# Two neighbouring rows per partition in the experts' weight tiles, and attention scores of two heads by turns

## The chip, the cores and the metric

The kernel runs on one core of a Trainium2 chip. The metric is the device time of one execution in microseconds (us). Engines are named as in the profile: PE is the matrix engine and PEld its weight loads (LDWEIGHTS), DVE the vector engine, ACT the scalar engine, POOL the GpSimd, SP the engine that issues most DMAs. A core has 16 DMA engines.

## The reference

All data is float32, batch 1, 256 tokens of 1024 channels beside a context of 256 tokens. A first block (Fourier mixer and state-space mixer) is followed by a second block of two layers, and it is the second block that the change touches:

```
for l in range(2):                      # layer 0 also updates the context stream, layer 1 does not
    sh1, sc1, g1, sh2, sc2, g2 = split(silu(c) @ ada_w[l] + ada_b[l], 6)   # the same for the context
    h  = rms_norm(x, norm_mix[l]) * (1 + sc1) + sh1
    x  = x + g1 * (even_layer if l == 0 else odd_layer)(h, hc)
    h2 = rms_norm(x, norm_ffn[l]) * (1 + sc2) + sh2
    x  = x + g2 * expert_choice_ffn(h2, router[l], w1[l], w3[l], w2[l])
...
even_layer:  4 differential heads (two softmaxes each, over 64 channels) and 8 neighbourhood heads of 64
             channels with an added bias; queries of x see keys of x and of the context, those of the context its own
odd_layer:   8 latent-attention heads, and 4 retention heads of 64 key and 128 value channels
expert_choice_ffn:   16 experts, each takes its 32 best tokens of a stream
    hid = silu(xe @ w1[e]) * (xe @ w3[e]);   ye = (hid @ w2[e]) * gate      # w1, w3, w2 are 1024 x 1024
```

Three matrices of 4 MiB for each of 16 experts in two layers make 384 MiB of weights, each read once: that is 403 MB of the 557 MB that the kernel moves.

## The kernel before

The program is one long list of Python generators that are woven into each other (`weave`), after which a scheduler orders each engine's instructions. SP issues the weight loads in program order; a load waits until the buffer that it fills has been read.

**Experts** (`moe`, from L1144). For each expert, `ffn` (L1256) multiplies the 32 chosen tokens by a 1024 x 1024 matrix. `load_m` (L1242) brings the matrix as four tiles of 1 MiB, `w` [128 partitions, 2, 1024], where partition p of tile `kk` holds rows 128·2kk + p and 128·(2kk+1) + p of the matrix: two runs of 4 KiB that lie 512 KiB apart in memory. PE keeps the tokens (`lhs`, columns of `xe`, `xf` or `hidT`) and streams the weights. In layer 0 the 64 columns of two streams are kept (x and context) and the array's columns serve two halves of the output, in layer 1 it is 32 columns and four quarters. Buffers for these tiles come from every pool that is free at the time (`slots`), about 20 of them.

The tokens that an expert reads, with their channels on partitions, are gathered by matmuls (`gather`, L1187): 128 channels of x, scaled, are the kept operand, and a 0/1 matrix is streamed. Channel block k is columns 128k to 128k + 127. Each block is then scaled and shifted by columns that `ada` (L359) computed. After w1 and w3, `hid` is transposed on PE in blocks of 128 columns (L1309) to be the kept operand for w2. `route` (L1081) transposes x in the same blocks for the router's logits.

**Even layer** (`even_attend`, L1370). It runs first for the context (`Qc`), woven with the projections of x, then for x (`Qx`), woven with the context's output projection. `scores` (L1375) multiplies the queries of one head, 64 partitions, by the keys: head 2ch + half lies on partitions 64·half to 64·half + 63, so that its matmul uses one half of the array's rows. For x there are two matmuls per head (own keys, context keys), and for a neighbourhood head a third, over all 128 rows, that adds the bias between the two. Then come the row maximum on DVE, the exponential on ACT, PE transposes and the matmul with the values.

**Ada** (`ada`): in the second block 12 calls per layer, each with two weight tiles [128, 4, 512] (runs of 2 KiB) and 32 matmuls on quarters of the array's columns.

**Prologue** (`late_rows`, L324): ten small DMAs issued by POOL and three PE transposes turn gain and bias vectors into columns (`VC`, `CV`; `BC` holds the ada biases).

Of the kernel before, what the change touches and what calls it, by code (L numbers as in the profile page):

```python
# [113 lines left out]
def kernel(ctx, tc, A, out, dbg=None):  # L114
# [25 lines left out]
    def psa():  # L140
        return ps_("a")
# [6 lines left out]
    def mm(o, l, r, start=True, stop=True, **kw):  # L148
        PE.matmul(o, l, r, start=start, stop=stop, **kw)  # L149
# [132 lines left out]
    v2 = pp.tile([128, 2, 128], F32, name="v2")  # L282
    v4 = pp.tile([128, 128], F32, name="v4")

    def rows_in(t, r0, ap, eng=G):
# [38 lines left out]
    def late_rows():  # L324
# [14 lines left out]
        V.tensor_copy(CV, p[:, 0:200])  # L339

    def vcol(name, i):
        c = VCI[name] + i
        return VC[:, c:c + 1]
# [5 lines left out]
    def ada_early(l, s, slots):  # L349
# [3 lines left out]
        for b in range(2):  # L353
# [3 lines left out]
            early[l, s].append(w)  # L357

    def ada(src, s, pair, cols, bias, between=None, bank=None, ws=None):  # L359

        p = (bank or psa)()
        for b in range(2):
            w = ws[b] if ws else load_w(src, [(s * 512, 512)], k0=4 * b, k=4)
            if between and b == 0:
                between()
            for k in range(4):
                for j in range(4):
                    mm(p[32 * j:32 * j + 32, 0:128], SC[:, 4 * b + k, pair, :], w[:, k, 128 * j:128 * j + 128],
                       start=b == 0 and k == 0, stop=b == 1 and k == 3)
# [142 lines left out]
    with tc.issue_after(after):  # L512
        late_rows()
    now(c2)
    pro.close()
# [541 lines left out]
    def router_rows(l):  # L1057
        nc.sync.dma_start(RW[l], A["moe_router_2"][l].rearrange("(k p) n -> p k n", p=128))

# [21 lines left out]
    def route(l, s, src, at="a", tag="b", jt="b"):  # L1081
# [5 lines left out]
        for kk in range(4):  # L1087
            xT = rowp.tile([128, 512], F32, name="xT", tag="r")
            p = ps_(TB[s])
            for j in range(2):  # L1090
                for t in range(2):
                    tr(p[:, 256 * j + 128 * t:256 * j + 128 * t + 128],
                       src[:, t, (2 * kk + j) * 128:(2 * kk + j + 1) * 128])
            if kk in (2,):
# [49 lines left out]
    def moe(l, streams, stk):  # L1144
# [42 lines left out]
        def gather(s, part, k, n=1):  # L1187
# [3 lines left out]
            if k % n == 0:  # L1191
                c = slice(128 * k, 128 * k + 128 * n)
                if n == 1:
# [48 lines left out]
        def load_m(src, k0, apart=False):  # L1242

            if not slots["first"]:
                slots["first"] += slots["all"]
            pool, tag = slots["first"].pop(0)
            w = pool.tile([128, 2048], F32, name="wm", tag=tag).rearrange("p (k n) -> p k n", k=2)
            sv = src.rearrange("(k p) n -> p k n", p=128)
            if apart:
                for k in range(2):  # L1250
                    nc.sync.dma_start(w[:, k], sv[:, k0 + k])
            else:
                nc.sync.dma_start(w, sv[:, k0:k0 + 2])
            return w
# [13 lines left out]
        def run():  # L1268
# [27 lines left out]
            for e in range(16):  # L1296
# [73 lines left out]
    def even_attend(st, Q, Y, nb_t=None):  # L1370
# [18 lines left out]
        for t in range(2):  # L1389
# [3 lines left out]
            for h in range(4):  # L1393
                pr = []
                for c in range(2):
                    ps = psa()
                    scores(ps, 0, h, c, qs)
                    pr.append(softmax_p(l2, ps, n, 1.0, "pr"))

# [17 lines left out]
            su8 = sm.tile([128, 8], F32, name="su8")  # L1417
            for h in range(8):
                ps = psa()
# [262 lines left out]
    def retention():  # L1682
# [11 lines left out]
        ps = psa()  # L1694
        for h in range(4):
            o = 64 * (h % 2)
            for d in range(2):
                c = 128 * (2 * d + h // 2)
                for t in range(2):
                    mm(ps[o:o + 64, c:c + 128], kw[:, t, d, 64 * h:64 * h + 64], rv[:, 2 + t, 128 * h:128 * h + 128],  # L1700
                       start=t == 0, stop=t == 1)
# [3 lines left out]
        for h in range(4):  # L1705
            o, a_ = slice(64 * (h % 2), 64 * (h % 2) + 64), h // 2
            ps = psa()
            for j in range(2):
                mm(ps[:, 256 * j:256 * j + 256], rkT[o, a_, 128 * j:128 * j + 128], rqT[o, a_, :])
            V.tensor_tensor(D[:, h], ps, D[:, h], op=OP.mult)  # L1710
            yield
        for t in range(2):
            qs = slice(128 * t, 128 * t + 128)
            cr = rs_.tile([128, 2, 2, 2, 128], F32, name="cr")
            for par in range(2):
                o = slice(64 * par, 64 * par + 64)
                ps = psa()
                for a_ in range(2):
                    for d in range(2):
                        c = 128 * (2 * d + a_)  # L1720
                        mm(ps[:, c:c + 128], rqT[o, a_, qs], sst[o, d, a_, :])
# [110 lines left out]
```

## Time and profile before

| | us |
|---|---|
| median of 3 executions | 1906.96 (1906.41 to 1912.91) |
| the profiled execution's own time | 1906.99 |
| its span, first to last instruction | 1905.1 |
| PE busy / DVE busy / ACT busy / POOL busy | 1652.3 / 794.4 / 519.3 / 335.1 |

The page of the profile lists 382 loads of 1024 KB for the experts' tiles and 4 of 512 KB, 18.4 us each (median) from issue to landing. The span falls into these stretches, by the tiles in use: first block to about 460 us, context attention to 600, x's attention to 740, experts of layer 0 from 760 to 1230, odd layer to 1430, experts of layer 1 from 1440 to 1892.

How to read it: a matmul of float32 operands stands in the trace as two records. A record's duration covers the array's depth too, so records overlap, and it is the distance between their starts that counts. "idle before" names what an engine waited for. The granted clock of PE is 1.00 for 2.4 GHz and 0.50 for 1.2 GHz, a mean over the stretch.

### The profile page before, as it was taken

Reading aid. Unit: us, or ns where it says so; the run is one execution under the profiler, and the core shown is the slowest. Engines: PE = TensorE matmul, PEld = TensorE weight load, DVE = VectorE, ACT = ScalarE, POOL = GpSimd, SP = SyncE. Lnnn points to the kernel's source line nnn. Section 1 sums busy time; section 2 is a strip of 40 time slices with the busy share of each in tenths; the row PEclk is TensorE's granted clock in tenths of the full one; section 3 lists DMA queues with packets and bytes.
Section 4 is the critical chain, followed back from the end, with each engine's and each line's share of the span. In section 5 each row is a group of like instructions: output and inputs, shape, how many; then the busy total and the mean of one; then the engine's idle time right before and its main releaser. Section 6 shows DMA issues by size and latency. Waiting matters only on the chain.

```text
span 1905.1 us, 29062 instructions
## 1 busy us (share of the span) xinstructions
PE 1652.3 (87%) x12036; PEld 1026.2 (54%) x12036; DVE 794.4 (42%) x1563; ACT 519.3 (27%) x1042; POOL 335.1 (18%) x288
## 2 busy tenths in 40 slices
PE   5999999899999998999989997789998966666665
PEld 4877777799887676433323322278784522222221
DVE  4538798947546655322323121164743300000002
ACT  4335555636443442211200000062532200000001
POOL 3114553633413310000000000041300000000001
PEclk8999999999999999999999999999997976776767
DMA  9576544555576539899989999951397999999996
GB/s 343 198 233 219 173 148 141 170 190 190 186 235 168 187 139 382 300 373 409 409 338 409 409 409 409 402 163 71 126 352 273 408 408 409 409 409 409 409 409 274
DMA packets 223016, 557.11 MB, mean 292 GB/s; under 512 B 23531, under 2 KB 80199, under 8 KB 222884
## 3 DMA queue, kind: packets, MB, share of 16 engines
q1 hardware_dynamic: 216608, 547.92, 76.9%
q10 hardware_dynamic: 5732, 6.26, 1.0%
q8 instruction: 95, 1.56, 0.3%
q0 software_dynamic: 544, 1.06, 0.1%
q14 instruction: 37, 0.30, 0.0%
HBM read 554.16 MB, written 1.05 MB: 291 GB/s over the span
## 4 chain that ended last, share of the span: by engine, by line
PE 60%; DMA 26%; DVE 8%; ACT 3%; issue 2%; POOL 1%; SPq 0%; DVEq 0%; POOLq 0%; ACTq 0%
PE ps_a L149 48%; DMA wm<-in_moe_w_dram 22%; PE ps_b L149 7%; PE ps_b L256 3%; DMA w<-in_w_in_dram 2%; DVE w L800 1%; PE ps_g L149 1%; DMA w<-in_w_ada_dram 1%; DVE wh L205 1%; ACT wh L203 1%; DMA w<-in_w_out_dram 1%; DVE ye L1323 1%; DVE pr L1404 1%; DVE hid L1305 1%; DVE acc L614 1%
## 5 line engine op out<-in xcount | busy, mean ns | idle before, releaser
L149 PE MATMUL ps_a<-wm,xf 128*32 128x256 f32 (+1 forms) x1792 | 280.0, 558 | 73.6 <-DMA wm<-in_moe_w_dram 71.8
L149 PE MATMUL ps_a<-wm,hidT 128*32 128x256 f32 (+1 forms) x1536 | 211.8, 529 | 47.4 <-DMA wm<-in_moe_w_dram 31.7
L149 PEld LDWEIGHTS ps_a<-wm,xf 128*32 128x32 f32 (+1 forms) x1792 | 90.4, 138 | 255.9 <-issue 133.3
L203 ACT ACTIVATE wh<-w 128x1024 fp32r<-128x1024 f32 (+3 forms) x152 | 151.7, 1007 | 164.6 <-PE ps_a L149 99.9
L1305 DVE TENSOR_TENSOR hid<-hid,ps_a 128x512 f32<-128x512 f32 (+1 forms) x32 | 17.7, 555 | 375.2 <-PE ps_a L149 375.2
L205 POOL TENSOR_TENSOR wh<-w,wh 128x1024 fp32r<-128x1024 f32 (+3 forms) x50 | 116.0, 2321 | 304.4 <-ACT wh L203 278.5
L205 DVE TENSOR_TENSOR wh<-w,wh 128x1024 fp32r<-128x1024 f32 (+3 forms) x102 | 135.2, 1329 | 71.9 <-ACT wh L203 71.4
L149 PEld LDWEIGHTS ps_a<-wm,hidT 128*32 128x32 f32 (+1 forms) x1536 | 70.4, 133 | 158.6 <-issue 74.8
L1323 DVE TENSOR_TENSOR ye<-ps_a,SC 32x512 f32<-32x512 f32 (+1 forms) x128 | 70.8, 553 | 193.9 <-PE ps_a L149 192.3
L1303 ACT ACTIVATE hid<-ps_a 128x512 f32<-128x512 f32 (+1 forms) x32 | 15.7, 490 | 480.9 <-PE ps_a L149 458.8
L149 PE MATMUL ps_a<-hT,wh 128*128 128x512 f32 (+1 forms) x672 | 136.3, 359 | 6.6 <-ACT hT L496 5.0
L1222 POOL TENSOR_TENSOR Pg<-Pg,CV 128x128 f32<-128x128 f32 x24 | 9.5, 421 | 748.7 <-DVE Pg L1220 748.7
L149 PEld LDWEIGHTS ps_a<-hT,wh 128*128 128x128 f32 x672 | 110.9, 197 | 25.9 <-ACT hT L496 5.4
L149 PE MATMUL ps_a<-E,wh 128*128 128x256 f32 x768 | 102.3, 288 | 6.1 <-DVE wh L205 2.5
L149 PE MATMUL ps_a<-wm,xe 128*32 128x256 f32 (+1 forms) x768 | 104.3, 481 | 0.7 <-ACT hid L1303 0.5
L149 PEld LDWEIGHTS ps_a<-E,wh 128*128 128x128 f32 x768 | 95.1, 192 | 12.6 <-issue 3.2
L149 PE MATMUL ps_a<-wh,E 128*128 128x256 f32 (+1 forms) x576 | 100.9, 326 | 0.1
L149 PEld LDWEIGHTS ps_a<-wh,E 128*128 128x128 f32 x576 | 81.5, 188 | 12.6 <-issue 5.0
L149 PE MATMUL ps_a<-wm,ye 128*32 128x256 f32 x512 | 51.6, 543 | 25.5 <-DMA wm<-in_moe_w_dram 25.5
L614 DVE SCALAR_TENSOR_TENSOR acc<-ps_a,CV,acc 128x189 f32<-128x189 f32 (+2 forms) x160 | 66.7, 427 | 8.2 <-ACT acc L603 5.7
L1023 ACT ACTIVATE pr<-ps_a,nb 128x512 f32<-128x512 f32 (+1 forms) x80 | 48.0, 601 | 76.0 <-DVE nb L1020 63.8
L149 PE MATMUL ps_a<-w,SC 128*32 128x128 f32 x1728 | 64.4, 281 | 2.7 <-DMA w<-in_w_ada_dram 2.1
(525 smaller groups left out, 2416.4 us busy)
## 6 DMA issues: line engine op xcount, KB each, us to landing
wm<-in_moe_w_dram SPq DMA_DIRECT2D x382, 1024.0 KB, 18.4
w<-in_ada_w_dram SPq DMA_DIRECT2D x46, 1024.0 KB, 5.8
w<-in_even_w_in_dram SPq DMA_DIRECT2D x24, 1024.0 KB, 6.4
w<-in_w_ada_dram SPq DMA_DIRECT2D x12, 1024.0 KB, 8.9
w<-in_w_in_dram SPq DMA_DIRECT2D x8, 1024.0 KB, 7.4
w<-in_even_w_out_dram SPq DMA_DIRECT2D x8, 1024.0 KB, 6.8
w<-in_w_in_dram SPq DMA_DIRECT2D x12, 512.0 KB, 7.3
w<-in_w_in_dram SPq DMA_DIRECT2D x8, 768.0 KB, 4.4
```

Source lines behind the costliest of these rows:

```text
L149: PE.matmul(o, l, r, start=start, stop=stop, **kw)
L203: S.activation(hv, wv, AF.Copy)
L205: (G if flip_lo[0] == 0 else V).tensor_tensor(lo, wv, hv, op=OP.subtract)
L256: PE.transpose(o, i, ident[:n, :n])
L614: V.scalar_tensor_tensor(o, xi[:, r0 + dr:r1 + dr, c0 + dc:c1 + dc], tap(i, j), o, op0=OP.mult, op1=OP.add)
L800: V.scalar_tensor_tensor(w[:, r], cb[:, c, 1], dt[:, c, 24 + h:25 + h], w[:, r], op0=OP.mult, op1=OP.add)
L1023: S.activation(pr[:, :n], ps[:, :n], AF.Exp, bias=nb, scale=scale, accum_out=su)
L1222: G.tensor_tensor(g_, g_, bcast(AFF[s][:, t, e4, None], [128, 4, 32]), op=OP.mult)
L1303: S.activation(hid, p1[:, :N], AF.Silu)
L1305: V.tensor_tensor(hid, hid, p3[:, :N], op=OP.mult)
L1323: V.tensor_tensor(ye[o:o + 32, s, N * j:N * j + N], py[i:i + 32, :N], G2[i:i + 32, :], op=OP.mult)
L1404: V.scalar_tensor_tensor(pr[0][0][:, :n], pr[1][0][:, :n], rc, pr[0][0][:, :n], op0=OP.mult, op1=OP.add)
```

## The change

The rows of the experts' matrices are dealt out in another way: partition p of a tile holds rows 256m + 2p and 256m + 2p + 1, which is one run of 8 KiB. The channels that meet them must then be taken two apart, which `in_pairs` does in the gather, the hidden transposes and the router's transposes; the shift and scale columns are made in that order by `ada` for four of the twelve calls per layer, and their biases, the gain and the router's rows by new small loads (`pair_rows`, `router_rows`). In the even layer and in retention the matmuls of two heads are issued by turns, one on each half of the array's rows.

```
+    def pair_rows():                       # called behind late_rows(), in the prologue
+        ab = A["ada_b_2"]
+        for l in range(2):
+            rows_in(v5, 8 * l, ab[l:l + 1, 3072:5120].rearrange("o (m c) -> (o m) c", c=256))
+        rows_in(v5, 16, A["norm_ffn_2"].rearrange("l (m c) -> (l m) c", c=256))
+        p = psb()
+        for i in range(2):
+            tr(p[:, 24 * i:24 * i + 24], v5[:, i::2])
+        pv = p[:, 0:48].rearrange("p (i r) -> p i r", i=2)
+        for l in range(2):
+            V.tensor_copy(BC[:, 48 + 48 * l:64 + 48 * l].rearrange("p (m i) -> p i m", i=2), pv[:, :, 8 * l:8 * l + 8])
+        V.tensor_copy(VC[:, o:o + 16].rearrange("p (m i) -> p i m", i=2), pv[:, :, 16:24])
+    def in_pairs(j, n=128):
+        c = 256 * (j // 2) + j % 2
+        return slice(c, c + 2 * n - 1, 2)
...
     def ada(src, s, pair, cols, bias, between=None, bank=None, ws=None):
+        paired = pair == 1 and 6 <= s < 10
-                    mm(p[32 * j:32 * j + 32, 0:128], SC[:, 4 * b + k, pair, :], w[:, k, 128 * j:128 * j + 128],
+                    mm(p[32 * j:32 * j + 32, 0:128], SC[:, 4 * b + k, pair, :],
+                       w[:, k, in_pairs(j) if paired else slice(128 * j, 128 * j + 128)],
...
     def router_rows(l):
-        nc.sync.dma_start(RW[l], A["moe_router_2"][l].rearrange("(k p) n -> p k n", p=128))
+        nc.sync.dma_start(RW[l].rearrange("p (m i) n -> p m (i n)", i=2), A["moe_router_2"][l].rearrange("(m p i) n -> p m (i n)", p=128, i=2))
...
     def route(...):
-                    tr(p[:, 256 * j + 128 * t:256 * j + 128 * t + 128],
-                       src[:, t, (2 * kk + j) * 128:(2 * kk + j + 1) * 128])
+                    tr(p[:, 256 * j + 128 * t:256 * j + 128 * t + 128], src[:, t, in_pairs(2 * kk + j)])
...
         def gather(s, part, k, n=1):
-                c = slice(128 * k, 128 * k + 128 * n)
+                c = in_pairs(k) if n == 1 else slice(128 * k, 128 * k + 128 * n)
...
-                    c = 128 * (k % n)
-                    mm(ps, pair[s][i][:, t, c:c + 128], Ps[s][:, t], start=t == 0 and i == 0, stop=t == 1 and i == 1)
+                    c = slice(0, 128) if n == 1 else in_pairs(k % n)
+                    mm(ps, pair[s][i][:, t, c], Ps[s][:, t], start=t == 0 and i == 0, stop=t == 1 and i == 1)
...
         def load_m(src, k0, apart=False):
-            sv = src.rearrange("(k p) n -> p k n", p=128)
+            sv = src.rearrange("(m p i) n -> p m i n", p=128, i=2)[:, k0 // 2]
...
-                nc.sync.dma_start(w, sv[:, k0:k0 + 2])
+                nc.sync.dma_start(w, sv)
...
-                    tr(pt[:, 128 * c:128 * c + 128], hid[:, 128 * c:128 * c + 128])
+                    tr(pt[:, 128 * c:128 * c + 128], hid[:, in_pairs(c)])
...
-        def scores(ps, kind, ch, half, qs, bias=None):
-            hs_ = slice(64 * half, 64 * half + 64)
+        def scores(kind, ch, qs, bias=None):
+            pss = [psa(), psa()]
+            hs_ = [slice(64 * c, 64 * c + 64) for c in range(2)]
+            for c in range(2 if bias is not None else 0):
+                mm(pss[c][:, 0:256], flipm, bias[c], stop=False)
             for i, kv in enumerate(KVs):
-                b = bias is not None and i == 0
-                o = ps[:, 256 * i:256 * i + 256]
-                mm(o, Q[hs_, 4 * kind + ch, qs], kv[hs_, kind, 256 * ch:256 * ch + 256], stop=not b)
-                if b:
-                    mm(o, flipm, bias, start=False)
+                for c in range(2):
+                    mm(pss[c][:, 256 * i:256 * i + 256], Q[hs_[c], 4 * kind + ch, qs],
+                       kv[hs_[c], kind, 256 * ch:256 * ch + 256], start=i > 0 or bias is None)
+            return pss
...
-            for h in range(8):
-                ps = psa()
-                scores(ps, 1, h // 2, h % 2, qs, None if nb_t is None else nb_t[:, t, h])
-                pr, su = softmax_p(l2, ps, n, 1.0, "pr")
-                G.tensor_copy(su8[:, h:h + 1], su)
-                values(po[:, 64 * h:64 * h + 64], transposed(l2, pr, nk), 1, 64 * h)
-                yield
+            for hh in range(4):
+                prs = [softmax_p(l2, ps, n, 1.0, "pr")
+                       for ps in scores(1, hh, qs, None if nb_t is None else [nb_t[:, t, 2 * hh + c] for c in range(2)])]
+                for c, (pr, su) in enumerate(prs):
...
```

The differential heads and the three matmul groups of `retention` (L1682) are turned round in the same way.

The order in which the built programs issue shows what becomes of this. First PE in the context's attention, where `KV,Q` are score matmuls and `E`, `wh` the projections of x that are woven in; before:

```order
L149 MATMUL ps_a<-E_4479,wh 128x256
L149 MATMUL ps_a<-KV,Q 128x256
L149 MATMUL ps_a<-E_4479,wh 128x256
L149 MATMUL ps_a<-E_4480,wh 128x256
L149 MATMUL ps_a<-E_4479,wh 128x256 x2
```

and of the change:

```order
L149 MATMUL ps_a<-E_4489,wh 128x256
L149 MATMUL ps_a<-KV,Q 128x256 x2
L149 MATMUL ps_a<-E_4489,wh 128x256
L149 MATMUL ps_a<-E_4490,wh 128x256
L149 MATMUL ps_a<-E_4489,wh 128x256 x2
```

A head's score matmul that stood alone now stands beside that of the head on the other half of the rows. Second, PE in the attention of x, two neighbourhood heads (`KV_4530` and `KV_4540` are the keys of x, `nb_t` the bias, each `ps_a` number a head), before:

```order
L256 MATMUL ps_b_6465<-kb_73,pr_6461 128x128 x4
L149 MATMUL ps_a_6514<-KV_4530,Q_4531 128x256
L149 MATMUL ps_a_6514<-nb_t_6183,kb_73 128x256
L149 MATMUL ps_a_6514<-KV_3456,Q_4531 128x256
L149 MATMUL ps_a_6537<-KV_4530,Q_4531 128x256
L149 MATMUL ps_a_6537<-nb_t_6183,kb_73 128x256
L149 MATMUL ps_a_6537<-KV_3456,Q_4531 128x256
L149 MATMUL ps_b_6451<-KV_4530,prT_6470 128x64 x2
```

and of the change:

```order
L256 MATMUL ps_b_6486<-kb_73,pr_6475 128x128 x4
L149 MATMUL ps_a_6524<-nb_t_6193,kb_73 128x256
L149 MATMUL ps_a_6524<-KV_4540,Q_4541 128x256
L149 MATMUL ps_a_6524<-KV_3466,Q_4541 128x256
L149 MATMUL ps_a_6525<-nb_t_6193,kb_73 128x256
L149 MATMUL ps_a_6525<-KV_4540,Q_4541 128x256
L149 MATMUL ps_a_6525<-KV_3466,Q_4541 128x256
L149 MATMUL ps_b_6461<-KV_4540,prT_6491 128x64 x2
```

The bias moved to the front of each head; the two heads follow one another, not by turns. Third, SP, where `wm` are the experts' tiles:

```order
-L1253 DMA wm<-in_moe_w_2_dram 128x2x1024 x6
-L1058 DMA kb<-in_moe_router_dram 128x8x16
-L1253 DMA wm<-in_moe_w_2_dram 128x2x1024
+L1280 DMA wm<-in_moe_w_2_dram 128x2048 x6
+L1086 DMA kb<-in_moe_router_dram 128x4x32
+L1280 DMA wm<-in_moe_w_2_dram 128x2048
```

SP's loads keep their places; the shape of the tiles' runs is other.

## Rows read from the trace of the kernel before

**Rows 1.** The page: DMA's busy share and rate in 40 slices.

```profile
DMA  9576544555576539899989999951397999999996
GB/s 343 198 233 219 173 148 141 170 190 190 186 235 168 187 139 382 300 373 409 409 338 409 409 409 409 402 163 71 126 352 273 408 408 409 409 409 409 409 409 274
```

**Rows 2.** The page: the chain that ended last, by line.

```profile
PE ps_a L149 48%; DMA wm<-in_moe_w_dram 22%; PE ps_b L149 7%; PE ps_b L256 3%; DMA w<-in_w_in_dram 2%; DVE w L800 1%; PE ps_g L149 1%; DMA w<-in_w_ada_dram 1%; DVE wh L205 1%; ACT wh L203 1%; DMA w<-in_w_out_dram 1%; DVE ye L1323 1%; DVE pr L1404 1%; DVE hid L1305 1%; DVE acc L614 1%
```

**Rows 3.** Stretches of the experts: busy us (instructions) by engine, clock, DMA, GB/s.

```profile
770.00:970.00 200.00, 190.57 (x819) 73.58 (x819) 65.02 (x146) 40.46 (x103) 5.83 (x8) 0.98 0.94 367
970.00:1230.00 260.00, 226.33 (x982) 73.63 (x980) 49.78 (x80) 9.38 (x16) 3.88 (x10) 1.00 1.03 409
1460.00:1886.00 426.00, 298.17 (x3058) 119.60 (x3050) 52.92 (x133) 23.74 (x59) 3.66 (x9) 0.75 1.02 408
```

**Rows 4.** PE's waits, 970 to 1240, then 1520 to 1895: total, times, longest.

```profile
PE ps_a L149 <- DMA wm<-in_moe_w_dram: 17.0, 26, 1.2
...
PE ps_a L149 <- DMA wm<-in_moe_w_dram: 112.0, 117, 2.9
```

**Rows 5.** The chain in order of time, first DMA pieces of either layer.

```profile
1095.42 18.51 DMA wm<-in_moe_w_dram
...
1518.98 18.42 DMA wm<-in_moe_w_dram
```

**Rows 6.** Stretches with runs of 2 KiB, then of 1 KiB, in flight.

```profile
0.00:14.00 14.00, 3.13 (x38) 2.06 (x38) 0.57 (x4) 3.94 (x7) 2.35 (x9) 1.00 0.85 313
14.00:18.00 4.00, 4.00 (x45) 3.48 (x45) 1.02 (x4) 2.99 (x5) 0.00 (x0) 1.00 1.03 388
424.00:428.00 4.00, 4.00 (x27) 3.55 (x26) 0.87 (x2) 1.11 (x2) 0.00 (x0) 1.00 1.07 357
```

**Rows 7.** SP's timeline: loads issued before those two stretches.

```profile
6.49 4.40 SPq L189 DMA_DIRECT2D w<-in_w_ada_dram  x2
...
412.93 32.86 SPq L189 DMA_DIRECT2D w<-in_even_w_in_dram  x7
```

**Rows 8.** PE's timeline in x's attention: start, us, instruction, records.

```profile
664.14 1.14 PE L149 MATMUL ps_a<-KV,Q 64*128 64x256 f32 x8
665.22 3.29 PE L149 MATMUL ps_a<-wh,E 128*128 128x512 f32 x13
...
690.45 0.70 PE L149 MATMUL ps_a<-KV,Q 64*128 64x256 f32 x2
691.07 0.70 PE L149 MATMUL ps_a<-nb_t,kb 128*128 128x256 f32 x2
691.70 0.70 PE L149 MATMUL ps_a<-KV,Q 64*128 64x256 f32 x4
692.33 0.70 PE L149 MATMUL ps_a<-nb_t,kb 128*128 128x256 f32 x2
...
693.59 1.10 PE L149 MATMUL ps_b<-KV,prT 128*128 128x64 f32 x8
```

**Rows 9.** Stretches of the even layer, columns as in Rows 3.

```profile
400.00:600.00 200.00, 197.81 (x1765) 173.41 (x1765) 111.78 (x229) 95.95 (x203) 62.64 (x56) 1.00 0.64 207
620.00:740.00 120.00, 118.95 (x752) 89.17 (x742) 70.98 (x150) 49.13 (x109) 27.77 (x31) 1.00 0.56 203
```

**Rows 10.** Prologue: the chain's DVE piece, DVE's copies, POOL's last DMA.

```profile
41.67 1.96 DVE MS L388
...
43.56 0.23 DVE L302 COPY SC<-ps_b 128x8 f32<-128x8 f32 x2
...
25.50 0.51 POOL L287 DMA_DIRECT2D v<-in_conv_b_dram  x1
```

**Rows 11.** Operands that the change reads two apart: weight loads, streamed ada weights.

```profile
L256 PEld LDWEIGHTS ps_t<-kb,hid x64: 138/141/143, 788.7 to 1227.9; 128*128 128x128 f32 x64
L149 PEld LDWEIGHTS ps_g<-P,xp x192: 186/189/333, 759.9 to 957.8; 128*128 128x128 f32 x192
...
22.16 1.95 PE L149 MATMUL ps_a<-w,SC 128*32 128x128 f32 x64
```

More of the change, by code (lines that the diff above doesn't have):

```diff
@@ L283 @@
     v4 = pp.tile([128, 128], F32, name="v4")
+    v5 = pp.tile([24, 256], F32, name="v5")
     def rows_in(t, r0, ap, eng=G):
@@ L339, in late_rows @@
         V.tensor_copy(CV, p[:, 0:200])
+    def pair_rows():
+        ab = A["ada_b_2"]
+        ab = ab if len(ab.shape) == 2 else ab.rearrange("o l n -> (o l) n")
+        for l in range(2):
[7 more added lines that the diff above has]
+            V.tensor_copy(BC[:, 48 + 48 * l:64 + 48 * l].rearrange("p (m i) -> p i m", i=2), pv[:, :, 8 * l:8 * l + 8])
+        o = VCI["norm_ffn_2"]
+        V.tensor_copy(VC[:, o:o + 16].rearrange("p (m i) -> p i m", i=2), pv[:, :, 16:24])
     def vcol(name, i):
@@ L513 @@
         late_rows()
+        pair_rows()
     now(c2)
@@ L1247, in load_m @@
             w = pool.tile([128, 2048], F32, name="wm", tag=tag).rearrange("p (k n) -> p k n", k=2)
-            sv = src.rearrange("(k p) n -> p k n", p=128)
+            sv = src.rearrange("(m p i) n -> p m i n", p=128, i=2)[:, k0 // 2]
             if apart:
                 for k in range(2):
-                    nc.sync.dma_start(w[:, k], sv[:, k0 + k])
+                    nc.sync.dma_start(w[:, k], sv[:, k])
             else:
-                nc.sync.dma_start(w, sv[:, k0:k0 + 2])
+                nc.sync.dma_start(w, sv)
             return w
@@ L1393, in even_attend @@
             for h in range(4):
-                pr = []
-                for c in range(2):
-                    ps = psa()
-                    scores(ps, 0, h, c, qs)
-                    pr.append(softmax_p(l2, ps, n, 1.0, "pr"))
+                pr = [softmax_p(l2, ps, n, 1.0, "pr") for ps in scores(0, h, qs)]
                 rc = sm.tile([128, 1], F32, name="rc", bufs=6)
@@ L1417, in even_attend @@
             su8 = sm.tile([128, 8], F32, name="su8")
-            for h in range(8):
-                ps = psa()
-                scores(ps, 1, h // 2, h % 2, qs, None if nb_t is None else nb_t[:, t, h])
-                pr, su = softmax_p(l2, ps, n, 1.0, "pr")
-                G.tensor_copy(su8[:, h:h + 1], su)
-                values(po[:, 64 * h:64 * h + 64], transposed(l2, pr, nk), 1, 64 * h)
-                yield
+            for hh in range(4):
+                prs = [softmax_p(l2, ps, n, 1.0, "pr")
+                       for ps in scores(1, hh, qs, None if nb_t is None else [nb_t[:, t, 2 * hh + c] for c in range(2)])]
+                for c, (pr, su) in enumerate(prs):
+                    h = 2 * hh + c
+                    G.tensor_copy(su8[:, h:h + 1], su)
+                    values(po[:, 64 * h:64 * h + 64], transposed(l2, pr, nk), 1, 64 * h)
+                    yield
             V.reciprocal(su8, su8)
@@ L1694, in retention @@
         ps = psa()
-        for h in range(4):
-            o = 64 * (h % 2)
+        for a_ in range(2):
             for d in range(2):
-                c = 128 * (2 * d + h // 2)
+                c = 128 * (2 * d + a_)
                 for t in range(2):
-                    mm(ps[o:o + 64, c:c + 128], kw[:, t, d, 64 * h:64 * h + 64], rv[:, 2 + t, 128 * h:128 * h + 128],
-                       start=t == 0, stop=t == 1)
+                    for h in (2 * a_, 2 * a_ + 1):
+                        o = 64 * (h % 2)
+                        mm(ps[o:o + 64, c:c + 128], kw[:, t, d, 64 * h:64 * h + 64], rv[:, 2 + t, 128 * h:128 * h + 128],
+                           start=t == 0, stop=t == 1)
         evac(sst, ps.rearrange("p (d a v) -> p d a v", d=2, a=2))
@@ L1704, in retention @@
         sd = D.rearrange("p h (j i) -> p h j i", j=2)
-        for h in range(4):
-            o, a_ = slice(64 * (h % 2), 64 * (h % 2) + 64), h // 2
-            ps = psa()
+        for a_ in range(2):
+            pss = [psa(), psa()]
             for j in range(2):
-                mm(ps[:, 256 * j:256 * j + 256], rkT[o, a_, 128 * j:128 * j + 128], rqT[o, a_, :])
-            V.tensor_tensor(D[:, h], ps, D[:, h], op=OP.mult)
-            yield
+                for par in range(2):
+                    o = slice(64 * par, 64 * par + 64)
+                    mm(pss[par][:, 256 * j:256 * j + 256], rkT[o, a_, 128 * j:128 * j + 128], rqT[o, a_, :])
+            for par in range(2):
+                h = 2 * a_ + par
+                V.tensor_tensor(D[:, h], pss[par], D[:, h], op=OP.mult)
+                yield
         for t in range(2):
@@ L1714, in retention @@
             cr = rs_.tile([128, 2, 2, 2, 128], F32, name="cr")
-            for par in range(2):
[L1716 to L1721, printed above, removed]
+            pss = [psa(), psa()]
+            for a_ in range(2):
+                for d in range(2):
+                    c = 128 * (2 * d + a_)
+                    for par in range(2):
+                        o = slice(64 * par, 64 * par + 64)
+                        mm(pss[par][:, c:c + 128], rqT[o, a_, qs], sst[o, d, a_, :])
+            for par in range(2):
+                ps = pss[par]
                 dq = dec[:, 0, t].rearrange("p d (a b) -> p d a b", b=2)[:, :, :, par, None]
```

## The prediction

> **What bounds the kernel now.** I read the page's slices first. The DMA row has two long plateaus at 409 GB/s with a share of 9 tenths or more, in the second half of the span [rows 1]. The chain of waits says how much hangs on them: 48% of it is PE's work on `ps_a`, 22% is loads of the experts' tiles [rows 2]. Cut into stretches, the experts show three regimes [rows 3]. From 770 to 970 us PE is busy for 190.6 of 200 us and DMA moves 367 GB/s, so PE sets the pace. From 970 to 1230 DMA runs at 409 GB/s throughout while PE still has 226 of 260 us; from 1460 to 1886 it runs at 408 and PE, at a mean clock of 0.75, is busy for 298 of 426. PE waits for tiles 17.0 us in the first of these two and 112.0 us in the second [rows 4], and the chain goes through loads from 1095 and from 1519 on [rows 5]. So 260 + 426 = 686 us go at the rate of the 16 DMA engines. In the even layer it is PE: 197.8 of 200 us and 118.95 of 120 [rows 9].
>
> **The tiles' runs of 8 KiB.** Bytes, number of loads and their order on SP stay; a tile now has 128 runs of 8 KiB instead of 256 of 4 KiB. What a run's length is worth shows in three places where DMA is full. The experts' 4 KiB runs move at 409 GB/s. At 14 us 14 x 313 = 4.4 MB have passed [rows 6], which is the constants (0.4 MB) and nearly four tiles of 1.05 MB; the two that follow are ada tiles with 2 KiB runs [rows 7], at 388 GB/s. From 424 to 428 only projections with 1 KiB runs are in flight, at 357. One engine's time for a run is its bytes x 16 / rate: 45.9, 84.5 and 160.2 ns for 1, 2 and 4 KiB. Twice the shorter less the longer is a fixed part per run: 2 x 45.9 - 84.5 = 7.3 and 2 x 84.5 - 160.2 = 8.8 ns. With 8 ns, 8 KiB take 2 x 160.2 - 8 = 312.4 ns, or 419.6 GB/s. The ends: if an engine handles a long run in pieces of 4 KiB, 409. If the time per further KiB goes on falling as it does in the rows (38.6, then 37.9, so 37.1 ns), 8 KiB take 308.6 ns, 425 GB/s. A lower rate has no row for it; the pieces are the same bytes of the same 1 MiB. I take 419.6, since two pairs of rows give nearly the same fixed part.
>
> The gain is then 426 x (1 - 409/419.6) = 10.8 us in layer 1 and 260 x 0.0253 = 6.6 us in layer 0. From 770 to 970 I count nothing: a faster load finds its next buffer still being read. In 970 to 1230 PE's 226 us leave 34, more than the 6.6 asked for.
>
> The Trainium skill has a rule against this term: in "DMA: Bandwidth & Descriptors", section Specifications, a transfer reaches line rate from 512 B per run on. By it 1, 2, 4 and 8 KiB would all go at one rate, and the sum would lack the 17.4 us, which is the time of rival B. The trace disagrees for the three shorter lengths, 357, 388 and 409 GB/s; for 8 KiB no run here shows it.
>
> **The score matmuls.** Single rows price them [rows 8]. One matmul (two records) alone between matmuls of another row mode takes 0.63 us to the next start (690.45 to 691.07); two on different halves take 0.63 together (691.70 to 692.33); four, two on each half, take 1.08 (664.14 to 665.22). So a slot costs 0.43 us, a run of such matmuls 0.20 on top, and halves run side by side even where they were not issued by turns. I counted runs and slots in the order of both programs. In the context's attention 26 runs with 28 slots become 18 with 18: the neighbourhood heads, alone before, now stand in pairs. That is 8 x 0.20 + 10 x 0.43 = 5.9 us; one run before is shared with x's first heads, so I take 8 x 0.63 = 5.0. In x's attention the scheduler does not alternate: each head has its bias first and then two matmuls on the same half. 37 runs with 46 slots become 26 with 54: -11 x 0.20 + 8 x 0.43 = +1.2 us. The net is -3.8 us; PE sets the pace in both, so I count it in full. If DVE, whose row maxima now come two at a time, takes the pace instead, it is 0. Retention's 7 runs become 6: nothing.
>
> "TensorEngine Tiling (Array Packing)" in the Trainium skill, section Theoretical Speedup, gives up to two for a contraction of 64 or less. By that alone the 96 score matmuls (32 + 64) would lose half of 96 x 0.43, 20 us, and the time be 1870. The rows agree with the factor and deny the gain: pairs that met ran at once already, and in x's attention they still don't meet.
>
> **New work.** The prologue gets three POOL DMAs at 0.51 us, issued by 27.5 us; the three transposes that they join run at 40.7, so their landing is covered. Three more DVE copies at 0.23 / 2 us stand between the pieces of DVE's chain [rows 10]: +0.4 us. The router's rows come in half as many runs, off the path. Operands taken two apart are read by PE in 32 + 64 hidden transposes, 48 of the router, 64 + 128 weight loads of the gather, and the streamed weights of 8 ada calls. No row shows PE reading in steps of two, so the ends are nothing and twice the time: 0.14 us for each of the 272 of these 336 loads that no DMA wait covers, and 8 x 1.95 us [rows 11], 38 + 16 = 54 us. A gain is excluded, as a step saves no element. I take nothing: the same number of elements passes, and these loads of 0.14 to 0.19 us mostly lie under a matmul of 0.27 us or more. ACT's and DVE's reads for the gather in layer 0 are stepped too; both are busy for a third of that stretch or less.
>
> **Sum.** The profiled execution took 1906.99 us, 1.9 more than its span and the same as the median. 1907.0 - 10.8 - 6.6 - 3.8 + 0.4 = 1886.2, so 1886 us.
>
> **Rivals.**
> A (forecast): as above. With the rate between 415 and 425 and the scores between 0 and 5 us it gives 1876 to 1897.
> B: the run's length is not what holds the rate; 409 GB/s stays. For it: no row is longer than 4 KiB, and each doubling brought less (31, then 21 GB/s). Against it: a fixed part of the same size from both pairs. Time: 1907.0 - 3.8 + 0.4 = 1903.6.
> C: in layer 0 PE takes over. For it: PE is busy 87% of 970 to 1230 and waits only 17.0 us for tiles; a PE that must first catch up what it lost before 970 may not use a faster load. Against it: 409 GB/s without a dip means that no load waited for a buffer. Time: 1886.2 + 6.6 = 1893.
> D, slower: PE reads two-apart operands at half speed, and the gather, which stands in PE's order between the experts' matmuls (192 and 128 loads), delays everything behind it. It decides once it exceeds the 21 us saved, that is from about 40% of the 54 us on; at its full price 1886 + 54 = 1940. For it: the stretch from 770 to 970 has no slack on PE. Against it: loads overlap matmuls, and all five kinds would have to be slow.
>
> **Chances.** A 0.60, B 0.20, C 0.10, D 0.08; the remaining 0.02 is a larger gain of the scores, half of 96 x 0.43 in place of 3.8, 1869. About 0.5% (9.5 us) is what a measurement can tell from no change, so faster means below 1897.4: A, C and the remainder, 0.72. The same is B, 0.20. Slower is D, 0.08. The range for 8 in 10 must take in A, C and B: 1873 to 1907. A's own is 1876 to 1897.
>
> **What would show it.** Right: the two plateaus at 417 to 422 GB/s and as many MB in about half as many packets; the stretch of layer 1 some 11 us shorter, that of layer 0 from its first full-rate load some 7. In the context's attention `KV,Q` rows with 4 records and 0.63 us to the next start. Rows of the hidden transposes' weight loads that still read 0.14 us. Wrong: plateaus at 409 (B), a dip in layer 0's plateau with PE above 95% (C), weight loads of 0.28 us or stepped ada calls of over 3 us (D).

## The result, and the profile after

The changed kernel takes 1889.74 us (median of 4 runs, 1885.52 to 1895.68) where the kernel before, on the same chip, takes 1909.93 (1906.41 to 1915.25): a ratio of 0.9894, 95% interval 0.9855 to 0.9933. A second comparison on another occasion gave 0.9887 (0.9866 to 0.9908). The execution that was profiled is the longest of the four, 1895.68 us with a span of 1893.6, so the two traces differ by 11.5 us where the medians differ by 20.2. Stage lengths below are therefore read from several profiles.

The page of the changed kernel has these slices of DMA, as [rows 1], and this count of packets:

```profile
DMA  9567544646575539789979999962386999999996
GB/s 346 193 213 236 170 133 144 200 151 222 178 234 155 222 112 372 301 357 420 421 304 421 422 421 421 418 188 73 112 328 265 419 420 419 420 419 420 420 421 258
DMA packets 173193, 557.13 MB, mean 294 GB/s; under 512 B 22580, under 2 KB 79272, under 8 KB 124165
```

Both plateaus stand at 418 to 422 GB/s in place of 409, and about 49,000 packets are 8 KiB or longer (173193 less 124165); the kernel before has 223016 packets, nearly all under 8 KiB. The slice at 304 is a dip that before had as well (338). Stretches as in [rows 3], shifted to where each plateau now lies:

```profile
980.00:1222.00 242.00, 218.09 (x940) 73.90 (x940) 47.33 (x74) 8.96 (x15) 3.23 (x8) 0.99 1.01 421
1460.00:1873.00 413.00, 281.46 (x3022) 116.88 (x3014) 52.92 (x133) 23.76 (x59) 3.70 (x9) 0.80 1.01 418
```

In layer 0 PE is now busy for 90% of a full plateau (before 87%). PE's waits for tiles from 970 to 1240 and from 1460 to 1880, then the first DMA pieces of the chain in either layer, against [rows 4, 5]:

```profile
PE ps_a L149 <- DMA wm<-in_moe_w_dram: 9.0, 17, 0.8
...
PE ps_a L149 <- DMA wm<-in_moe_w_dram: 115.3, 114, 2.3
```

```profile
1045.52 15.53 DMA wm<-in_moe_w_dram
...
1476.94 18.33 DMA wm<-in_moe_w_dram
```

The wait in layer 0 has nearly halved (17.0 before). The chain still runs on loads in both layers and meets its first one earlier, 1045 for 1095 and 1477 for 1519: what bounds the experts has not changed, it only moves faster. The page's chain by line says the same: loads have 30% where they had 22 [rows 2].

```profile
PE ps_a L149 40%; DMA wm<-in_moe_w_dram 30%; PE ps_b L149 7%; PE ps_b L256 3%; DMA w<-in_even_w_in_dram 2%; DVE w L828 1%; DMA w<-in_w_in_dram 1%; PE ps_g L149 1%; DVE wh L205 1%; DMA w<-in_w_ada_dram 1%; ACT wh L203 1%; DMA w<-in_even_w_ou
```

In the context's attention, two heads' scores now stand together (PE's timeline: start, us, instruction, records). Each group takes 0.63 to 0.64 us to the next start, as [rows 8] let expect:

```profile
517.83 0.70 PE L149 MATMUL ps_a<-KV,Q 64*128 64x256 f32 x4
518.47 1.41 PE L149 MATMUL ps_a<-wh,E 128*128 128x256 f32 x10
...
525.81 0.70 PE L149 MATMUL ps_a<-KV,Q 64*128 64x256 f32 x4
526.44 0.38 PE L149 MATMUL ps_a<-wh,E 128*128 128x256 f32 x1
```

But PE's waits are others. These are its lists from 600 to 705 us in full, of the kernel before and then of the changed one:

```profile
PE ps_b L256 <- DVE E L1046: 2.5, 1, 2.5
PE ps_b L256 <- DVE pr L1404: 1.0, 1, 1.0
```

```profile
PE ps_a L149 <- ACT wh L203: 3.2, 1, 3.2
```

Two waits for DVE are gone and one for ACT is new. ACT waits there for the load of the context's second projection tile. SP's timeline of the changed kernel shows when that was issued:

```profile
589.70 22.68 SPq L1471 DMA_DIRECT2D nb_t<-in_na_rpb_dram  x32
612.48 1.09 SPq L189 DMA_DIRECT2D w<-in_ada_w_dram  x2
613.62 1.23 SPq L1280 DMA_DIRECT2D wm<-in_moe_w_dram  x1
616.61 23.84 SPq L189 DMA_DIRECT2D w<-in_even_w_out_dram  x6
```

The tile is issued at 616.61 behind 32 small loads and 3 MiB of others, and ACT starts on it at 630.12. In the kernel before ACT starts on it at 630.16, and PE takes it at 633.0 without a wait; in the changed kernel PE stands from 628.0 on. ACT gets to the tile no later, PE is earlier. Behind the wait the granted clock of PE is lower, 0.50 from 631 to 636 us, where the kernel before has 1.00.

### The profile page after: what moved, and what is told of

Read it like the earlier page. It is cut to its first block, busy times and chain, and to the rows that moved or that the text cites. A ratio compares the mean times of both kernels' runs of the same rounds, so it can differ in the third digit from the quotient of the medians.

```text
span 1893.6 us, 29094 instructions
## 1 busy us (share of the span) xinstructions
PE 1641.4 (87%) x12038; PEld 1037.4 (55%) x12038; DVE 791.7 (42%) x1566; ACT 518.1 (27%) x1042; POOL 336.9 (18%) x291
## 2 busy tenths in 40 slices
DMA packets 173193, 557.13 MB, mean 294 GB/s; under 512 B 22580, under 2 KB 79272, under 8 KB 124165
## 4 chain that ended last, share of the span: by engine, by line
PE 51%; DMA 35%; DVE 8%; ACT 3%; issue 2%; POOL 1%; SPq 0%; POOLq 0%; DVEq 0%; ACTq 0%
PE ps_a L149 40%; DMA wm<-in_moe_w_dram 30%; PE ps_b L149 7%; PE ps_b L256 3%; DMA w<-in_even_w_in_dram 2%; DVE w L828 1%; DMA w<-in_w_in_dram 1%; PE ps_g L149 1%; DVE wh L205 1%; DMA w<-in_w_ada_dram 1%; ACT wh L203 1%; DMA w<-in_even_w_out_dram 1%; DVE ye L1350 1%; DVE acc L642 1%; DVE wh L787 0%
## 5 line engine op out<-in xcount | busy, mean ns | idle before, releaser
L149 PE MATMUL ps_a<-wm,xf 128*32 128x256 f32 (+1 forms) x1792 | 275.2, 551 | 72.1 <-DMA wm<-in_moe_w_dram 70.2
L149 PE MATMUL ps_a<-wm,hidT 128*32 128x256 f32 (+1 forms) x1536 | 204.6, 505 | 45.4 <-DMA wm<-in_moe_w_dram 29.0
L1330 ACT ACTIVATE hid<-ps_a 128x512 f32<-128x512 f32 (+1 forms) x32 | 15.7, 490 | 467.0 <-PE ps_a L149 445.8
L149 PE MATMUL ps_a<-wm,ye 128*32 128x256 f32 x512 | 46.8, 504 | 25.0 <-DMA wm<-in_moe_w_dram 25.0
```

The lines of the kernel that those rows point to most:

```text
L1330: S.activation(hid, p1[:, :N], AF.Silu)
```

## The experiments

Stage lengths in us, from first and last starts in the tile views: the first score matmul; from it to the first expert matmul; experts of layer 0 to their last hidden copy on DVE; the odd layer to ACT's first expert input of layer 1; experts of layer 1 to their last matmul.

| profile | first score | scores, router | layer 0 | odd layer | layer 1 |
|---|---|---|---|---|---|
| before | 467.4 | 296.4 | 464.5 | 210.7 | 451.0 |
| changed | 470.5 | 295.2 | 458.4 | 212.2 | 440.9 |
| changed, second profile | 469.5 | 292.9 | 458.9 | 214.8 | 441.1 |
| tiles only | 468.8 | 299.2 | 459.4 | 210.7 | 440.1 |
| turns only | 470.4 | 290.4 | 465.8 | 212.5 | 451.1 |
| 4 KiB runs | 468.5 | 288.9 | 467.0 | 213.5 | 452.6 |
| tied order | 469.0 | 303.4 | 459.2 | 210.3 | 440.6 |

### The tiles alone

The changed kernel with scores and retention as before:

```
     def scores(ps, kind, ch, half, qs, bias=None):      # as before
...
-            sv = src.rearrange("(k p) n -> p k n", p=128)
+            sv = src.rearrange("(m p i) n -> p m i n", p=128, i=2)[:, k0 // 2]
```

> The change without its second part: tiles with two neighbouring rows on a partition, scores and retention in the order of before. Theory T (the length of a tile's run sets the rate): plateaus at 420 to 421 GB/s, layer 1 about 10 us shorter than before and layer 0 about 6, less the prologue, so 13 to 17 us below the kernel before (ratio 0.991 to 0.993). Rival U (the turns bring it, the tiles little): within 4 us of before (ratio 0.998 to 1.002), whatever the plateaus show, because an earlier start of the experts is what moves the end. The prologue up to the first score matmul: if the three new small loads or the copies cost something there, that matmul starts 2 to 3 us later than in before here too, since this kernel has them; if the 3 us of the changed kernel's trace were chance, it starts within 1 us of 467.4.

Measured: 1898.12 us, ratio 0.9925 (0.9895 to 0.9955), which is 14.3 us below before by the ratio and 12.8 by the medians of all executions. Layer 0 is 5.1 us shorter, layer 1 10.9, the scores' stage 2.8 longer; all of that lies behind the last score matmul, and some 1.5 us of it are 64 ada matmuls at a lower clock, which "The changed kernel again" shows. Theory T holds, U falls. Its first score matmul is at 468.8, between the two expectations for the prologue.

### The turns alone

The kernel before with the changed `scores`, `even_attend` and retention.

> The kernel before with the scores and retention of the change alone, tiles as before. Theory T: the two attention stretches together 4 us shorter and nothing else, so 3 to 5 us below before (ratio 0.997 to 0.9985), plateaus at 409 GB/s. Rival U: 15 us or more below (0.992). Rival V (what the attention gains is given back where the experts wait for loads): within 1 us of before (1.000). Prologue as in before: the first score matmul at 467 to 468 us.

Measured: 1904.84 us, ratio 0.9954 (0.9936 to 0.9971): 8.8 us below before (6.1 by the medians), more than T's 3 to 5 but far from U's 15. In its profile the scores' stage is 6.0 us shorter; the first score matmul comes 3.0 later, at 470.4, though this kernel has none of the new work in the prologue, and layer 0 and the odd layer are 1.3 and 1.8 longer. So that one execution shows nothing of the gain at its end, partly as V has it; the median does. PE waits 3.5 us for ACT at the place where the changed kernel waits 3.2, and the kernel with the tiles alone does not: that wait belongs to the turns.

### Everything but the run's length

```
-                nc.sync.dma_start(w, sv)
+                nc.sync.dma_start(w[:, ::-1], sv[:, ::-1])
```

> The changed kernel with each tile's two rows loaded in reversed order on the source and on the tile, by one transfer as before it: same bytes, same layout in memory on both sides, same order of the program, but no run can be longer than one row, 4 KiB. Theory T (an engine pays some 8 to 9 ns for every run): plateaus back at 409 GB/s, as many packets as before, time 16 to 18 us above the changed kernel, 2 to 4 below before (ratio 0.998). Rival W (it is the neighbourhood of the two rows in DRAM that counts, not the length of one run): plateaus stay at 420, ratio 0.989. Rival X (a reversed order costs more than a plain 4 KiB run): plateaus below 405 and slower than before.

Measured: 1912.44 us, ratio 0.9995 (0.9974 to 1.0016). Packets and plateaus are those of before; the stretches of this kernel are

```profile
DMA packets 222088, 557.13 MB, mean 292 GB/s; under 512 B 22579, under 2 KB 79271, under 8 KB 221956
```

```profile
980.00:1222.00 242.00, 213.78 (x908) 70.70 (x906) 46.72 (x73) 8.36 (x14) 3.22 (x8) 0.99 1.03 409
1460.00:1886.00 426.00, 290.14 (x3026) 119.73 (x3018) 52.92 (x133) 23.72 (x59) 3.69 (x9) 0.78 1.02 408
```

Same bytes, same places in both memories, same order on PE: with the run at 4 KiB the plateaus are back at 409 and both layers of experts are at least as long as before (467.0 and 452.6). W and X fall. The two rows being neighbours brings nothing to the rate; the one long run does.

T's ratio of 0.998 lies within the interval. But this kernel has the turns, and the turns alone came out at 0.9954, with an interval that does not meet this one. So the rest of the change (operands two apart, the prologue, and here the reversed loads) takes back some 0.4%, and by the ratios the long run is worth about 1%, some 19 us (0.9995 against 0.9894), where T has 16 to 18.

### Rates by run length, and operands apart

None of the block's work is done here: loads of expert weights in groups of 16 MiB, and PE matmuls on one tile.

```
SY.dma_start(t.rearrange("p (k n) -> p k n", k=2), w.rearrange("(m p i) n -> p m i n", p=128, i=2)[:, q])   # 8 KiB
...
PE.transpose(ps[1][...], xt[:, 128 * i:128 * i + 128], ident)    # L172; L174 takes xt[:, i:i + 255:2], L176 xt[:, i:i + 509:4]
PE.matmul(ps[4][...], xt[:, 128 * i:128 * i + 128], xt[:, 512:640])   # L178; L180 loads, L182 streams two apart
```

> No part of the block is computed: eight groups of 16 loads of expert weights (16 MiB each; runs of 1, 2, 4, 8, 16, 32 KiB, then 4 KiB with two neighbouring rows in reversed order, then 8 KiB again), and behind them TensorE alone on one tile, with operands one, two and four elements apart. Theory T (a fixed part of about 8.5 ns per run on each of the 16 engines, 37.9 ns for each further KiB): 357, 388, 409, 421, 427 and 430 GB/s for 1 to 32 KiB, and 409 for the reversed rows. Rival W (neighbourhood in DRAM counts): 421 for the reversed rows. Rival B2 (the gain of the long run ends where it was measured): 16 and 32 KiB stay at 421 or fall below it. Weight loads: in the changed kernel's trace the transposes' loads of two-apart columns took 0.209 us, where they took 0.140, and their matmuls 0.283 where they took 0.273. If the step causes it, loads one apart take 0.14, two apart 0.21 and four apart more; if the place of the tile causes it, all three take the same. Streamed operands two apart: 0.27 us for 128 columns and 0.59 for 512, as one apart, if only loads feel the step; 0.28 and more otherwise.

The stretches inside the groups, in the order 1, 2, 4, 8, 16, 32 KiB, then 4 KiB reversed, then 8 KiB again (last two columns: DMA share, GB/s):

```profile
12.00:42.00 30.00, 0.00 (x0) 0.00 (x0) 0.00 (x0) 0.00 (x0) 1.00 1.10 348
57.00:85.00 28.00, 24.58 (x69) 12.09 (x70) 0.00 (x0) 0.00 (x0) 1.00 1.05 389
97.00:126.00 29.00, 29.00 (x84) 13.88 (x83) 0.00 (x0) 0.00 (x0) 1.00 1.03 409
137.00:167.00 30.00, 28.65 (x155) 19.89 (x153) 2.54 (x6) 0.00 (x0) 1.00 1.02 421
180.00:200.00 20.00, 0.00 (x0) 0.00 (x0) 0.00 (x0) 0.00 (x0) 0.50 1.01 430
222.00:242.00 20.00, 0.00 (x0) 0.00 (x0) 0.00 (x0) 0.00 (x0) 0.50 1.01 434
266.00:290.00 24.00, 0.00 (x0) 0.00 (x0) 0.00 (x0) 0.00 (x0) 0.50 1.03 410
300.00:330.00 30.00, 0.00 (x0) 0.00 (x0) 0.00 (x0) 0.00 (x0) 0.50 1.01 421
```

One engine's time for a run, bytes x 16 / rate, is 47.1, 84.2, 160.2, 311.3, 609.6 and 1208 ns. Twice the shorter less the longer gives 10.0, 8.2, 9.1, 13.0 and 11.2: the fixed part holds over the whole range. Theory T is right within 4 GB/s from 2 KiB on (1 KiB: 348 for 357), and B2 falls. The Trainium skill ("DMA: Bandwidth & Descriptors", section Specifications) has line rate from 512 B on and a ceiling of the fabric of 435 GB/s. The first is contradicted at every length here; the second agrees with the 434 of the longest run.

Weight loads of the same kernel (min/median/max ns):

```profile
L178 PEld LDWEIGHTS ps<-xt x64: 192/192/201, 88.2 to 143.3; 128*128 128x128 f32 x64
L180 PEld LDWEIGHTS ps<-xt x64: 196/197/201, 91.8 to 147.1; 128*128 128x128 f32 x64
...
L172 PEld LDWEIGHTS ps<-kb,xt x32: 139/140/142, 82.3 to 135.9; 128*128 128x128 f32 x32
L174 PEld LDWEIGHTS ps<-kb,xt x32: 194/207/209, 84.4 to 137.8; 128*128 128x128 f32 x32
L176 PEld LDWEIGHTS ps<-kb,xt x32: 208/211/213, 86.3 to 139.7; 128*128 128x128 f32 x32
```

and its matmuls (busy us, mean ns):

```profile
L182 PE MATMUL ps<-xt 128*128 128x128 f32 x64 | 7.7, 276 | 0.0
L178 PE MATMUL ps<-xt 128*128 128x128 f32 x64 | 7.5, 275 | 0.0
...
L174 PE MATMUL ps<-kb,xt 128*128 128x128 f32 x32 | 4.1, 282 | 0.0
L172 PE MATMUL ps<-kb,xt 128*128 128x128 f32 x32 | 3.8, 272 | 0.0
```

A transpose loads columns two apart in 207 ns, one apart in 140, four apart in 211, and its matmul takes 10 ns longer; a plain matmul's load takes 5 ns more, and what is streamed takes no more (276 for 275). So the step causes the longer loads of the changed kernel, but "four apart more" was wrong by all but 4 ns.

### The scores tied into one order

Each score matmul is put behind the one before it (`then`), both biases first:

```
+            def then(*args, **kw):
+                with (tc.issue_after(last[0].ins) if last[0] is not None else nullcontext()):
+                    last[0] = PE.matmul(*args, **kw)
```

> The changed kernel with the score matmuls of two heads tied into one order on TensorE (both biases, then half 0, half 1, half 0, half 1), since in x's attention the scheduler did not alternate. In the order there are now 22 runs with 39 slots in x's attention, in place of 26 with 54. Theory T (a slot costs 0.43 us, a run 0.20): 4 x 0.20 + 15 x 0.43 = 7.3 us less than the changed kernel, about 1882 where that has 1889.7 (ratio to before 0.985). Rival Y (TensorE then waits for the second bank, which DVE and ACT free one after the other): 0 to 2 us less, idle time before the score matmuls in its place. Rival Z: slower than the changed kernel by some us, as the tied order also holds up what the scheduler put between.

Measured: 1897.75 us, ratio 0.991 (0.9883 to 0.9938), not below the changed kernel. From start to start and less waits, the score matmuls of x's attention take 24.3 us where the changed kernel has 28.6, and the bias matmuls 7.8 for 8.9: they did get 5.4 us cheaper. The stage is 8.2 us longer all the same, and the tied kernel's list of PE's waits, 600 to 705 us, has most of the rest (10.5 us in all, 3.2 in the changed kernel):

```profile
PE ps_a L149 <- ACT wh L203: 5.2, 1, 5.2
PE ps_b L256 <- ACT pr L1051: 4.3, 3, 2.6
```

T is right on the direction of the matmuls (5.4 of 7.3 us) and wrong on the time. Y fits the second line; the first is the wait for the projection's tile again. In the median Y and Z can't be told apart, as the intervals overlap.

### Two attempts on the late tile

The first writes three steps of the context's projection ahead of the 32 bias loads (`for _ in range(3): next(op)`).

> The changed kernel, with the first three steps of the context's output projection written ahead of the loads of the position biases: its second weight tile is then issued on SP before those 32 transfers (22 us of SP) and not behind them. In the changed kernel's trace TensorE stands 3.2 us at 628 for this tile, which the kernel before did not, and its clock is low behind that (54 records of ada in 3.21 us, 2.29 in the trace of runs4k). Theory N (the turns made TensorE early enough to meet a late load, and so gave a part of their gain back): no wait for wh at 620 to 635, last score matmul 3 to 4 us after the first one earlier than in the changed kernel (228.0 us there), time 3 to 5 us below it. Rival M (x's attention is then limited by DVE's row maxima and softmax anyway, which start no earlier): the wait moves to pr or prT and the time stays within 1 us of the changed kernel. Rival L: the projection's matmuls, now ahead, make the first scores of x late, and it is slower by 2 us or more.

Measured: 1901.03 us, ratio 0.9929 (0.991 to 0.9949), slower than the changed kernel beside it (0.9887). N is wrong, and the time is L's. In this kernel's waits, 560 to 790 us, the wait has moved and grown:

```profile
PE ps_b L149 <- ACT prT L156: 7.9, 1, 7.9
```

ACT's own timeline explains it: at 617.7 ACT comes to a split of the projection's third tile and stands 8.08 us for its load, and the copy that PE needs is queued behind that.

```profile
625.76 2.00 ACT L203 ACTIVATE wh<-w 128x1024 fp32r<-128x1024 f32 x2 [8.08 <-DMA w<-in_even_w_out_dram]
627.67 0.58 ACT L156 ACTIVATE prT<-ps_b 128x512 f32<-128x512 f32 x1
```

The second attempt leaves SP's queue free: `G.dma_start(nb_t[...])` in place of `nc.sync.dma_start`.

> The changed kernel with the 32 small transfers of the position biases issued by POOL in place of SP; the order on TensorE stays. In the changed kernel SP spends 589.7 to 612.5 on issuing them, and behind them stand two ada tiles and one expert tile (3 MiB), all issued at 612.5 to 614.9, right ahead of the projection's second weight tile, which is issued at 616.6 and lands after 13.5 us; TensorE waits 3.2 us for it (3.7 in the second profile). Theory N2 (the 3 MiB ahead of it delay it): the three tiles go some 20 us sooner, the second weight tile lands within 6 to 8 us of its issue, the wait for wh at 628 is gone, and the time is 3 to 5 us below the changed kernel (ratio to before about 0.987 where that has 0.9887 to 0.9894). Rival M2 (the wait goes, but x's attention is then paced by softmax): wait for pr in its place, time within 2 us of the changed kernel. Rival Q (POOL's transfers are slower, and the biases come too late or stand in front of others): slower.

Measured: 1920.27 us, ratio 1.0049 (1.0032 to 1.0067); Q is right. PE's waits of this kernel from 460 to 790 us begin with

```profile
PE ps_a L149 <- ACT wh L203: 9.8, 1, 9.8
PE ps_a L149 <- POOL nb_t L1475: 4.9, 1, 4.9
```

The 3 MiB did go earlier, and the tile still came too late for PE (issued at 611.4, on ACT at 623.6): from 600 to 620 us DMA is busy with a share of 1.03 and moves 207 GB/s. N2 is not confirmed. Nor is the attempt as clean as its expectation says: the scheduler reordered PE in x's attention as well. What would make that tile early enough stays open; a version faster than the changed kernel was not found.

### The changed kernel again

> The changed kernel itself once more, beside the same runs of the kernel before, for a second profile and a time to compare the other one with. Theory C (the 2 to 3 us that its first profile lost up to the first score matmul, and the slow ada matmuls at 742, were chance): first score matmul between 467 and 471, the 64 records of ada at 742 in about 2.3 us where they took 3.9, ratio 0.987 to 0.991. Rival S (two-apart streamed operands are slow there): those records again at 415 ns and 3.9 us.

Measured: 1892.73 us, ratio 0.9887 (0.9866 to 0.9908), first score matmul at 469.5. The 64 ada records at 739 are slow again, 415 ns, so C is wrong there. But S is not shown by that: the kernel with 4 KiB runs and the first attempt on the late tile stream the same two-apart operand in 275 and 276 ns. What goes with the slow ones is the granted clock, 0.59 from 738 to 742 us, the lower level for most of it; the first attempt has 1.00 there:

```profile
738.00:742.00 4.00, 4.00 (x63) 3.31 (x62) 2.42 (x6) 1.45 (x4) 0.47 (x1) 0.59 1.02 424
```

```profile
758.00:761.00 3.00, 3.00 (x67) 2.65 (x68) 2.24 (x4) 1.24 (x3) 0.00 (x0) 1.00 0.99 410
```

PE had no long wait before the clock fell, one of 0.56 us in 20 us. Why the clock falls there in four of six profiles with 8 KiB tiles and in none of three with 4 KiB was not settled; it costs about 1.5 us (3.9 for the 64 records, 2.4 elsewhere).

## Why the prediction was right, point by point

**The rate**, 419.6 GB/s forecast: 418 and 421 in the kernel's two plateaus, 421 in the loads alone, and 409 again when the run is cut. Right, and by the mechanism named. The fixed part of 8 ns was 8.2 to 10.0 up to 8 KiB.

**Layer 1**, -10.8 us: -10.1, -9.9 and -10.9 in three profiles. Right. **Layer 0**, -6.6: -6.1, -5.6 and -5.1. Right, a little large. Against the kernel with 4 KiB runs, which differs in the run alone, it is -8.6 and -8.1 there and -11.7 and -11.5 in layer 1 (two profiles): the long run may have gained more than forecast, and the rest of the change lost some of it. Rival C had its condition half met (PE at 90% of the plateau), but its dip did not come.

**The scores**, -3.8: the step that was mis-sized. Take the distances from start to start without waits, and count the run that the context's last score matmul shares with x's first ones as the prediction does. Then the score matmuls fell from 17.4 to 11.7 us in the context's attention (-5.7; forecast -5.9, or -5.0 with 0.9 taken off for that run) and rose from 27.2 to 28.6 in x's (+1.4, forecast +1.2): -4.3 together. That run stands on the context's side before and on x's side in the changed kernel, so nothing was to be taken off. The 16 bias matmuls, which the working left out, fell from 9.9 to 8.9. That makes -5.3; the stage became 6.0 us shorter with the turns alone, and the time 8.8 (5.5 to 12.2).

The working also asked only whether DVE would take the pace, and not what else PE waits for. Two waits for DVE, 3.5 us, went; one for a load's tile came, 3.2 us in the changed kernel, 3.7 in its second profile, 3.5 with the turns alone, with a lower clock behind it. That the changed kernel keeps less of the gain in this stage (-1.2 and -3.5) than the turns alone (-6.0) is not due to that wait, which both have. From the start of the last score matmul to the first expert matmul it takes 67.2 and 67.3 us, the turns alone 64.8; some 1.5 us of the difference is the slow ada. The first profile lost another 2.4 between its first and last score matmul.

**The prologue**, +0.4: not shown. The first score matmul stands at 467.4 and 470.4 in the two kernels without the new work, and at 468.5 to 473.2 in the seven profiles with it. The 3.1 us between the first two traces are thus mostly spread, and a cost of some 1 us can't be excluded; in both traces a load of `w_in` is in the chain at 48 us, 7.14 us long in before and 8.36 in the changed kernel.

**Operands two apart**, 0 chosen of 0 to 54: the sign set for it failed. The hidden transposes' loads do not "still read 0.14":

```profile
L256 PEld LDWEIGHTS ps_t<-kb,hid x64: 194/209/223, 791.0 to 1223.7; 128*128 128x128 f32 x64
```

A cost of half again was real, and the reason given for nothing (the same number of elements passes) was wrong; the other reason, that loads lie under matmuls, carried the result. From start to start 54 hidden transposes of layer 0 take 8.5 us where they took 7.5; at these 19 ns, 96 hidden and 48 router transposes cost an estimated 2.7 us before any wait covers them. The gather's loads stayed at 0.19 us and the streamed ada weights at 0.27 where the clock was full. D, which needs over 21, falls.

**The sum.** 1886.2 forecast, 1889.7 and 1892.7 measured, 1895.7 in the profiled run. Against the trace of before that run has +3.1 to the first score, -1.2 in the scores' stage (new wait and slow ada included), -6.1, +1.5 in the odd layer, -10.1, and +1.3 behind the last expert matmul: -11.5. The parts alone, -14.3 and -8.8, add up to -23.1 (-12.8 and -6.1 by the medians, -18.9), and both together gave -20.2; the intervals cover the difference. That the sum came so near (-20.8 forecast) is in part luck, as its terms were off in opposite ways. By the ratios, the run's length is worth some 19 us (forecast 17.4) and the turns 8.8 (3.8), and what the change adds besides takes back an estimated 5 (from the tiles alone) to 8 (from the 4 KiB runs), where the forecast has 0.4; each of these figures is uncertain by some 4 us or more. Where those 5 to 8 us go is open: the profile of the kernel with 4 KiB runs is only 1.9 us above that of the turns alone, and its reversed loads may cost something outside the plateaus. Why the odd layer varies from 210 to 215 us stays open.

## What to carry to other kernels

Where a stage is held by full DMA engines, plot one engine's time per run against the run's length: here every run paid some 8 to 13 ns from 1 to 32 KiB, and a layout that doubles the run is worth that, without moving a byte less. Where PE gets faster in a stage that it paces, it meets other waits: here one for a load that it had never reached too soon; look for it in the issuing queue before counting the gain in full. Tying an order by hand made the matmuls 5.4 us cheaper and the stage 8.2 us longer, with 10.5 us of PE's waits where there were 3.2. And a near sum proves none of its terms: a run that keeps all of a change but one part prices that part and the rest.

## What had not been expected of the hardware

- The issue itself got cheaper. SP's issue of an expert tile takes 2.3 us (median) in the kernel before, 0.33 in the changed one, and 2.3 again with runs cut to 4 KiB. Full queues go with it: among the loads that were run alone, the first with 1 KiB runs is issued in 0.44 us and the median of its group in 2.9, while those with 16 and 32 KiB runs take 0.33 throughout. The cause itself was not tested.

```profile
L1253 SPq DMA_DIRECT2D wm<-in_moe_w_dram x382: 367/2301/7160, 612.2 to 1868.6; - x191
```

```profile
L1280 SPq DMA_DIRECT2D wm<-in_moe_w_dram x382: 327/328/1227, 613.6 to 1852.0; - x191
```

- A float32 transpose loads columns two apart half again as slowly (207 for 140 ns), and four apart hardly more slowly than two (211), while streaming two apart costs nothing (276 for 275).
- 32 small loads moved from SP's queue to POOL's, with the order that the scheduler then chose, cost 1.6% against the changed kernel (ratios 1.0049 and 0.9887).
